# adaLN modulation on four column quarters of TensorE, and grouped small matmuls, in a two-layer token mixer

## The chip, the cores and the metric

One NeuronCore of one Trainium2 chip runs the whole program. The metric is the device time of one execution in microseconds. All engines of the core (TensorE for matmuls, VectorE, ScalarE, GpSimd, SyncE for DMA queues) run side by side, each through its own list of instructions in order.

## What is computed

The reference is a two-layer hybrid block on 256 context and 256 latent tokens of width 1024. In each layer a modulation vector is computed from the conditioning vectors, then four token mixers (retention, RG-LRU, gated DeltaNet, RWKV-7) run side by side on the normed and modulated stream, their outputs are merged through gates and an output matrix, and a SwiGLU feed-forward part follows:

```python
for l in range(DEPTH):                       # DEPTH = 2
    ml = jnp.split(cond_lat @ mod_w[l] + mod_b[l], 6, axis=-1)   # silu(c), 1024 -> 6 x 1024
    mc = jnp.split(cond_ctx @ mod_w[l] + mod_b[l], 6, axis=-1)
    pl = split_projection(modulate(rms_norm(h_lat, norm1_g[l]), ml[0], ml[1]) @ in_w[l])
    pc = split_projection(modulate(rms_norm(h_ctx, norm1_g[l]), mc[0], mc[1]) @ in_w[l])
    ...
    h_lat = h_lat + ml[2] * y_lat
    h_lat = h_lat + ml[5] * swiglu(modulate(rms_norm(h_lat, norm2_g[l]), ml[3], ml[4]), ...)
```

The modulation is thus a product of two columns (context, latent) with a 1024 x 6144 matrix per layer, in six parts q of 1024. Parts 0 and 1 are needed in the first norm, part 2 after the output matrix, 3 and 4 in the second norm, 5 after the feed-forward part.

## The kernel before

Dense weights come from HBM in units of 128 x 1024 fp32 (512 KB, tile `raw`, line 382, on SP's queue). ScalarE casts a unit to fp32r (`wh`, line 391) and VectorE subtracts (`wl`, line 352), and a block of 128 x 128 is then multiplied in three fp32r matmuls of 512 columns: wh with the high part of the activations, wh with the low part, wl with the high part (`dense`, `inp`). The activations lie transposed, channels on partitions, as XH and XL.

The tasks of each layer stand in lists written out by `_phases` (line 116). `first` holds the modulation needed at once, `seq1` the RWKV, retention and LRU work between projections and gates (`ga`), `seq2` the gated DeltaNet heads (`gd`) with the merges (`mg`), `seqo` the eight output blocks (`ow`), and `seqf` two times eleven feed-forward input steps (`fi`) and eight output blocks (`fo`). The program is emitted in that order. A scheduler then sets the order of each engine's list, from dependences, priorities and its own costs, so that pieces of one task stand among those of others; weight loads and splits are emitted with a higher priority (`early`) and go as far ahead as their buffers allow.

`mod` (line 569) does one half of a part q, 512 columns. Four halves at the start are done unsplit: eight fp32 matmuls with the two conditioning columns, padded to 32, as stationary operand (`sc32`) and the weights moving. All others are split: sixteen fp32r matmuls with `schl` stationary (hi and lo columns) and wh or wl moving. They occupy the first 32 columns of the array. A transpose on VectorE and five adds put the result into MODS. Two split halves stand in `seq1` (q=2), four in `seqo` (q=3, 4), fourteen in `seqf` of layer 0 (q=5, and all of layer 1). Every split half takes 4 units through the wh/wl path.

`rw_half` (line 707) does one RWKV pair of heads on 256 tokens: four small products with `sw` for decay and rate, then four chunks jj one after the other. In a chunk the state ST gives `pr` (tile ch), the inverse SF gives `pu`, then `uv` with `kt` gives the state's addition pS, and the output Y collects ST with RA and uv with sc. The two heads e and directions d give four small matmuls for each. `inv16` (line 667) inverts 16 x 16 triangular blocks by steps of shuffle, multiply and add on VectorE; `gd_head` (line 1001) calls it with two lanes, one for each direction. `params` (line 512 on) derives per-layer constants on VectorE, for both layers in the first phase.

Of the kernel before, what the change touches and what calls it, by code (L numbers as in the profile page):

```python
# [10 lines left out]
F32 = mybir.dt.float32  # L11
# [29 lines left out]
_GCOLS = [("triF", 128), ("triB", 128), ("aftF", 128), ("aftB", 128), ("gout", 256), ("s16", 32), ("nm0", 1), ("nm1", 1)]  # L41
# [13 lines left out]
def _consts():  # L55
# [14 lines left out]
    C["s16"][:, 0:16] = -1.0 * (r16 < c16)  # L70
    C["s16"][:, 16:32] = -1.0 * (r16 > c16)
    C["nm0"][:, 0] = -1.0 * ((p % 32) < 16)
    C["nm1"][:, 0] = -1.0 * ((p % 32) >= 16)
# [30 lines left out]
def _mod(l, *parts):  # L104
    return [("mod", l, q, c) for q in parts for c in range(2)]
# [10 lines left out]
def _phases(l):  # L116

    last = l + 1 == DEPTH
    first = [("mod", 0, q, c) for c in range(2) for q in range(2)] if l == 0 else []
    if last:  # L120
        seq1 = [("rws",), ("kvr", 0), ("kvr", 1), ("rw", 0), ("rt", 0), ("lr", 0), *_ga(3, 0, 2), ("kvr", 2), ("rw", 1), ("rt", 1), ("lr", 1), *_ga(3, 2, 4), ("kvr", 3), ("rw", 2), ("rt", 2), ("lr", 2), *_ga(3, 4, 6), ("rw", 3), ("rt", 3), ("lr", 3), *_ga(3, 6, 8)]
    else:
        seq1 = [("rws",), ("kvr", 0), ("kvr", 1), ("rw", 0), ("rt", 0), ("lr", 0), *_mod(0, 2), *_ga(3, 0, 2), ("kvr", 2), ("rw", 1), ("rt", 1), ("lr", 1), *_ga(3, 2, 4), *_ga(0, 0, 2), ("kvr", 3), ("rw", 2), ("rt", 2), ("lr", 2), *_ga(3, 4, 6), *_ga(0, 2, 4), ("rw", 3), ("rt", 3), ("lr", 3), *_ga(3, 6, 8), *_ga(0, 4, 8), *_ga(2, 0, 4)]
# [15 lines left out]
    seqo += []  # L139
    seqf += []  # L140
# [34 lines left out]
def _blocks(task, ahead):  # L175
# [6 lines left out]
    if k == "mod":  # L182
        _, l, q, c = task
        for kk in range(8):
            out += [(("mod_w", l), kk, slice(1024 * q + 512 * c + 128 * j, 1024 * q + 512 * c + 128 * j + 128)) for j in range(4)]
        return out
# [25 lines left out]
def _pack(inp):  # L212
# [36 lines left out]
    for n, (l, (m, kk, cols)) in enumerate(plan):  # L249
        w = f["mod_w"][m[1]] if isinstance(m, tuple) else mats[m][l]  # L250
        W[n // 8, :, n % 8, :] = w[128 * kk:128 * kk + 128, cols]
# [3 lines left out]
    for l in range(DEPTH):  # L255
# [7 lines left out]
        "W": W.reshape(nu, 128, 1024),  # L263
        "P": P,
# [6 lines left out]
class Kern:  # L271
    def __init__(self, ctx, tc, ap, out, dbg=None, depth=DEPTH, upto=None):
        self.ctx, self.tc, self.nc, self.ap, self.out = ctx, tc, tc.nc, ap, out
        self.dbgo, self.depth, self.upto = dbg or {}, depth, upto
        self.n = self.wi = self.nd = 0

# [67 lines left out]
    def mm(self, out, lhsT, rhs, start=True, stop=True, chk=False):  # L344
        self.nc.tensor.matmul(out=out, lhsT=lhsT, rhs=rhs, start=start, stop=stop, skip_group_check=chk)  # L345
# [32 lines left out]
    def raw(self, u, pool=None):  # L378
        pool = pool or self.wps[u % len(self.wps)]
        with self.early():  # L380
            raw = self.tl(pool, [128, 1024], "raw", bufs=self.nraw if pool is not self.wps[0] else 2)
# [81 lines left out]
    def setup(self):  # L463
# [36 lines left out]
        self.schl = self.cp.tile([128, 8, 64], F32R, name="schl")  # L500
        self.act(self.schl, self.kc[:, 0:1].unsqueeze(2).to_broadcast([128, 8, 64]), AF.Copy, scale=0.0)
        self.nc.scalar.copy(self.schl[:, :, 0:2], self.sc)
        self.nc.scalar.copy(self.schl[:, :, 32:34], self.sc)
        self.tt(self.schl[:, :, 2:4], self.sc, self.schl[:, :, 0:2].bitcast(F32), ALU.subtract)
# [6 lines left out]

    def params(self, l):
        nc = self.nc
        d = self.tl(self.cp, [128, 160], "dp", bufs=2)
# [5 lines left out]

        self.omu, self.hmu = col(15), col(15)
        self.ts(self.omu, self.p("mu", 0, 15), -1.0, 1.0, ALU.mult, ALU.add)
        self.ts(self.hmu, self.p("mu", 0, 15), 0.5)
# [45 lines left out]
    def mod(self, l, q, c, split=True):  # L569

        ps = self.psd()[0:32]
        for k in range(8):
            if not split:
                if k % 2 == 0:
                    u = self.wi // 8
                    _, raw = self.raw(u, self.wps[u % 3 != 2])
                    self.wi += 8
# [1028 lines left out]
```

## Time and profile before

| | us |
|---|---|
| runs of the kernel before: median (lowest, highest) | 2492.82 (2486.88, 2495.9) |
| the profiled execution, its own time | 2479.02 |
| span of the profiled execution | 2477.2 |
| TensorE busy, matmuls | 2358.9 |
| VectorE busy | 1767.9 |
| ScalarE busy | 1124.1 |

The span runs from the first to the last instruction in the profile; the execution's own time holds a little more. Busy TensorE time comes from modelled ends of matmuls that overlap, so the distance from start to start is what a matmul costs where the engine is full.

### The profile page before, as it was taken

What the parts mean: (1) busy time and instruction counts of PE and PEld (TensorE: products, weight loads), DVE (VectorE), ACT (ScalarE), POOL (GpSimd) and SP (SyncE); (2) the same over time, 40 slices, a digit from 0 to 9 for tenths busy, and PEclk for the clock granted to TensorE, in tenths of its full rate; (3) what the DMA queues carried; (4) which work ended last, traced back from release to release, by engine and by line L of the source; (5) the groups of instructions that cost most, each with busy time, mean ns of one, the idle gap of its engine ahead of it and who ended that gap; (6) DMA issues with size and microseconds to landing.
All of it is one profiled execution on the core that took longest, in us unless ns stands there. A gap on an engine that the chain in (4) does not pass through costs nothing. (4 is left out here: it accounts for less than half of the span.)

```text
span 2477.2 us, 48500 instructions
## 1 busy us (share of the span) xinstructions
PE 2358.9 (95%) x19016; PEld 1873.1 (76%) x19016; DVE 1767.9 (71%) x5357; ACT 1124.1 (45%) x2129; POOL 48.1 (2%) x146
## 2 busy tenths in 40 slices
PE   7999999999999999989999989999999999988998
PEld 2766777676877877667787877777777887888998
DVE  5787859685599965777635446978887688966555
ACT  3455445454444433444423224556564444544443
POOL 0000000000000000000000000000000000000000
PEclk9999999999999999999999999989999989989999
DMA  6214121212523243646635332212121432454553
GB/s 233 84 50 125 44 98 52 70 52 79 167 80 101 83 138 135 212 138 219 213 94 186 94 103 91 68 56 72 60 74 53 126 95 91 122 190 142 183 183 111
DMA packets 91381, 282.77 MB, mean 114 GB/s; under 512 B 10512, under 2 KB 21008, under 8 KB 90768
## 3 DMA queue, kind: packets, MB, share of 16 engines
q1 hardware_dynamic: 86256, 271.62, 34.2%
q10 hardware_dynamic: 4896, 8.05, 1.0%
q8 instruction: 150, 2.46, 0.4%
q14 instruction: 79, 0.65, 0.1%
HBM read 262.85 MB, written 16.78 MB: 113 GB/s over the span
## 5 line engine op out<-in xcount | busy, mean ns | idle before, releaser
L345 PE MATMUL d<-XH,wh 128*128 128x512 f32 (+1 forms) x2112 | 763.5, 363 | 22.9 <-ACT XH L342 10.8
L391 ACT CAST wh<-raw 128x1024 fp32r<-128x1024 f32 x436 | 452.2, 1048 | 721.8 <-PE d L345 473.8
L345 PE MATMUL d<-XL,wh 128*128 128x512 f32 (+1 forms) x2112 | 764.1, 362 | 2.9 <-DVE XL L359 2.9
L345 PE MATMUL d<-XH,wl 128*128 128x512 f32 (+1 forms) x2112 | 760.2, 360 | 0.8 <-DVE wl L352 0.8
L352 DVE TENSOR_TENSOR wl<-raw,wh 128x1024 fp32r<-128x1024 f32 x436 | 528.6, 1223 | 294.0 <-ACT wh L391 289.3
L345 PEld LDWEIGHTS d<-XH,wh 128*128 128x128 f32 x2112 | 403.0, 191 | 89.4 <-ACT XH L342 15.2
L345 PEld LDWEIGHTS d<-XL,wh 128*128 128x128 f32 x2112 | 404.0, 191 | 62.2 <-DVE XL L359 5.9
L345 PEld LDWEIGHTS d<-XH,wl 128*128 128x128 f32 x2112 | 404.3, 191 | 58.5 <-issue 7.5
L359 DVE SCALAR_TENSOR_TENSOR t<-t,d 128x512 f32<-128x512 f32 (+1 forms) x136 | 74.8, 551 | 83.8 <-PE d L345 75.3
L345 PE MATMUL d<-ih,wh 128*128 128x512 f32 (+1 forms) x352 | 118.3, 336 | 0.0
L345 PE MATMUL d<-il,wh 128*128 128x512 f32 (+1 forms) x352 | 118.3, 336 | 0.0
L345 PE MATMUL d<-ih,wl 128*128 128x512 f32 (+1 forms) x352 | 118.3, 336 | 0.0
L345 PE MATMUL d<-yh,wh 128*128 128x512 f32 (+1 forms) x256 | 92.1, 368 | 11.0 <-ACT yh L430 4.7
L345 PE MATMUL d<-yl,wh 128*128 128x512 f32 (+1 forms) x256 | 94.0, 368 | 3.2 <-DVE yl L352 3.2
L345 PE MATMUL d<-yh,wl 128*128 128x512 f32 (+1 forms) x256 | 91.2, 359 | 0.0
L359 DVE SCALAR_TENSOR_TENSOR H<-d,MOD,H 128x256 f32<-128x256 f32 x72 | 32.8, 479 | 55.2 <-PE d L345 55.0
L345 PEld LDWEIGHTS d<-ih,wl 128*128 128x128 f32 x352 | 66.8, 190 | 6.9
L345 PEld LDWEIGHTS d<-ih,wh 128*128 128x128 f32 x352 | 66.8, 190 | 6.9
L345 PEld LDWEIGHTS d<-il,wh 128*128 128x128 f32 x352 | 66.8, 190 | 6.8
L345 PE MATMUL d<-wh,schl 128*32 128x512 f32 x160 | 63.8, 400 | 2.1 <-DVE t L359 0.8
L345 PE MATMUL d<-wl,schl 128*32 128x512 f32 x160 | 65.4, 408 | 0.0
L345 PEld LDWEIGHTS d<-yh,wh 128*128 128x128 f32 x256 | 51.9, 206 | 16.7 <-ACT yh L430 5.7
(356 smaller groups left out, 3730.1 us busy)
## 6 DMA issues: line engine op xcount, KB each, us to landing
raw<-in_W_dram SPq DMA_DIRECT2D x452, 512.0 KB, 3.7
gd<-tm SPq DMA_DIRECT2D x20, 256.0 KB, 2.9
t<-gd SPq DMA_DIRECT2D x20, 256.0 KB, 4.2
yt<-yd SPq DMA_DIRECT2D x16, 256.0 KB, 4.5
H<-in_xT_dram ACTq DMA_DIRECT2D x8, 256.0 KB, 6.7
lrw<-in_LW_dram ACTq DMA_DIRECT2D x8, 256.0 KB, 2.6
yd<-tr SPq DMA_DIRECT2D x8, 256.0 KB, 3.4
H<-in_xT_dram SPq DMA_DIRECT2D x1, 2048.0 KB, 11.1
```

The lines of the kernel that those rows point to most:

```text
L345: self.nc.tensor.matmul(out=out, lhsT=lhsT, rhs=rhs, start=start, stop=stop, skip_group_check=chk)
L352: self.nc.vector.tensor_tensor(out=out, in0=a, in1=b, op=op)
L359: self.nc.vector.scalar_tensor_tensor(out=out, in0=a, scalar=s, in1=b, op0=op0, op1=op1)
L391: self.nc.scalar.copy(wh, r3)
```

## The change

The modulation is no longer split and no longer done in halves. A part q is eight steps k; a step loads 128 x 1024 fp32 of a repacked matrix WM (tile `mraw`, line 592, SP's queue), and four fp32 matmuls multiply 256 columns each, every one on its own 32 columns of the array and into its own 32 partitions of one PSUM tile (printed as `mg`). One transpose and one add end a part. The steps are grouped into tasks of n steps, and a new helper `gang` ties the matmuls of a task together: every later one of a group gets a dependence without a semaphore on the first, which is the one that is loaded last. The parts are placed anew: q=1, 0 and 2 in the first phase with a pool of 16 steps, q=3 and 4 as eight tasks of two steps after the output blocks with a pool of two steps, q=5 and layer 1's six parts as fourteen tasks of four steps in the feed-forward part with a pool of eight.

In `rw_half` the sw products write two PSUM tiles with both x side by side, and `gang` holds together sw, KB with RA, pr with ST's part of Y, pu, and pS with uv's part of Y. `gd_head` transposes the second direction's blocks first and runs one lane of eight blocks. Layer 1's parameters are loaded and derived at the sixth step of the feed-forward part, layer 0's after `rw_shared`, and the first few (`params_mu`) before it.

```diff
+def _mod(l, n, *parts):
+    return [("mod", l, q, k, n) for q in parts for k in range(0, 8, n)]
...
-    first = [("mod", 0, q, c) for c in range(2) for q in range(2)] if l == 0 else []
+    first = _mod(0, 1, 1, 0) + _mod(0, 4, 2) if l == 0 else []
...
-    mo = [] if last else _mod(0, 3, 4)
+    mo = [] if last else _mod(0, 2, 3, 4)
...
-    mf = [] if last else _mod(0, 5) + _mod(1, 0, 1, 2, 3, 4, 5)
+    mf = [] if last else _mod(0, 4, 5) + _mod(1, 4, 0, 1, 2, 3, 4, 5)
...
-            seqf += [("fi", f, j)] + mf[:1]
-            mf = mf[1:]
+            seqf += [("fi", f, j)]
+            if j and len(mf) > 2:
+                seqf += mf[:1]
+                mf = mf[1:]
         seqf += [("fo", f, m) for m in range(8)]
+    seqf += mf
...
     def mm(self, out, lhsT, rhs, start=True, stop=True, chk=False):
-        self.nc.tensor.matmul(out=out, lhsT=lhsT, rhs=rhs, start=start, stop=stop, skip_group_check=chk)
+        i = self.nc.tensor.matmul(out=out, lhsT=lhsT, rhs=rhs, start=start, stop=stop, skip_group_check=chk).ins
+        if self.ganged is not None:
+            if self.ganged:
+                self.tc.add_manual_dep(i, self.ganged[0].name, mybir.DependencyInfo(mybir.DependencyClass.NoSync, mybir.DependencyReason.DATA), reason="gang")
+            self.ganged.append(i)
...
+    def mod(self, l, q, k0, n):
+        W = []
+        for k in range(k0, k0 + n):
+            with self.early():
+                w = self.tl(self.mq, [128, 1024], "mraw")
+                self.nc.sync.dma_start(out=w, in_=self.ap["WM"][l, q, k])
+            W.append((k, w))
+        if k0 == 0:
+            self.mps = self.psm()
+        with self.gang():
+            for x, (k, w) in enumerate(W[::-1]):
+                for j in range(4):
+                    self.mm(self.mps[32 * j:32 * j + 32, 0:256], self.sc32[:, k], w[:, 256 * j:256 * j + 256],
+                            start=(k0 + x == 0), stop=(k0 + x == 7))
+        if k0 + n == 8:
+            t = self.t2(256)
+            self.nc.vector.transpose(out=t, in_=self.mps[:, 0:256])
+            self.tt(self.MODS[l][:, 8 * q:8 * q + 8, :], t.rearrange("p (m r) -> p m r", r=32)[:, :, 0:2],
+                    self.modb[:, l, 8 * q:8 * q + 8].unsqueeze(2).to_broadcast([128, 8, 2]), ALU.add)
...
+            with self.gang():
                 for d in range(2):
                     for e in range(2):
-                        self.mm(pS[E_[e], d], kt[:, d, jj, 64 * e:64 * e + 64], uv[:, jj, d, e])
+                        if not last:
+                            self.mm(pS[E_[e], d], kt[:, d, jj, 64 * e:64 * e + 64], uv[:, jj, d, e])
+                if out:
+                    for d in range(2):
+                        rv = slice(None, None, -1) if d else slice(None)
+                        t = slice(64 * ch(jj, d), 64 * ch(jj, d) + 64)
+                        for e in (1, 0):
+                            self.mm(Y[E_[e], t], uv[:, jj, d, e], sc[:, e, jj, d, 64:128][:, rv], start=False, stop=(jj == 3 and d == 1), chk=True)
...
-        self.inv16([(Nc[:, 0], Sc[:, 0], True), (Nc[:, 1], Sc[:, 1], False)], 4)
+        self.inv16([(U(Nc), U(Sc), True)], 8)
```

First place: SP's list at the start. `raw` is a unit of weights, `mraw` a step of the modulation. Before, the last units of the modulation, then the dense ones:

```order
L382 DMA raw_259<-in_W_dram 128x1024
L382 DMA raw_263<-in_W_dram 128x1024
L382 DMA raw_267<-in_W_dram 128x1024
L382 DMA raw_271<-in_W_dram 128x1024
L382 DMA raw_549<-in_W_dram 128x1024
L382 DMA raw_579<-in_W_dram 128x1024
L382 DMA raw_620<-in_W_dram 128x1024
```
Now the first rows, then the last step of q=0 with the first of q=2, then the last of q=2 with the dense units after it:

```order
L592 DMA mraw_155<-in_WM_dram 128x1024
L391 DMA raw_421<-in_W_dram 128x1024
L592 DMA mraw_162<-in_WM_dram 128x1024
L391 DMA raw_451<-in_W_dram 128x1024
...
L592 DMA mraw_276<-in_WM_dram 128x1024
L592 DMA mraw_344<-in_WM_dram 128x1024
...
L592 DMA mraw_375<-in_WM_dram 128x1024
L391 DMA raw_658<-in_W_dram 128x1024
L391 DMA raw_692<-in_W_dram 128x1024
```
Eight steps of q=2 moved in between q=0 and the dense units, and four dense units moved ahead, between the first steps.

Second place: TensorE's list in the second half of the first RWKV pair, where the chunk's uv is used (d is a dense PSUM tile, XH and XL the activations, x an LRU product, ch the state's addition). Before:

```order
L345 MATMUL d_2257<-XH,wh_2260 128x512
L345 MATMUL d_2257<-XL,wh_2260 128x512
L345 MATMUL Y_1628<-sc_1385,uv_1387 64x64
L345 MATMUL d_2257<-XH,wl_2261 128x512
L345 MATMUL d_2257<-XH,wh_2260 128x512
L345 MATMUL ch_1693<-uv_1387,kt_1386 64x64 x4
L345 MATMUL Y_1628<-sc_1385,uv_1387 64x64 x3
L345 MATMUL x_2140<-lrx_2050,lrw_2048 128x512
L345 MATMUL d_2257<-XL,wh_2260 128x512
```
And now at the same chunk:

```order
L343 MATMUL d_2119<-XL,wh_2122 128x512
L343 MATMUL d_2119<-XH,wl_2123 128x512
L343 MATMUL x_2098<-lrx_2008,lrw_2006 128x512
L343 MATMUL ch_1625<-uv_1345,kt_1344 64x64 x4
L343 MATMUL Y_1586<-sc_1343,uv_1345 64x64 x4
L343 MATMUL d_2153<-XH,wh_2156 128x512
L343 MATMUL d_2153<-XL,wh_2156 128x512
L343 MATMUL d_2153<-XH,wl_2157 128x512
```
The four products of Y, of which one stood apart from the others before, stand behind those of ch.

Third place: TensorE's list at the end of the output stage, and SP's within it. On TensorE the first row belongs to the last task of q=4; mg with a new number is q=5, st are the norm's row sums and their broadcast, d with XH the first feed-forward matmuls:

```order
L343 MATMUL mg_10639<-mraw_10771,sc_112 32x256 x4
L343 MATMUL mg_11053<-mraw_11051,sc_112 32x256 x4
L343 MATMUL mg_11053<-mraw_11049,sc_112 32x256 x4
L343 MATMUL mg_11053<-mraw_11047,sc_112 32x256 x4
L343 MATMUL mg_11053<-mraw_11045,sc_112 32x256 x4
L343 MATMUL mg_11053<-mraw_11144,sc_112 32x256 x4
L343 MATMUL mg_11053<-mraw_11142,sc_112 32x256 x4
L343 MATMUL mg_11053<-mraw_11140,sc_112 32x256 x4
L343 MATMUL mg_11053<-mraw_11138,sc_112 32x256 x4
L343 MATMUL st_10814<-cstt,t_1957_10791 128x1 x4
L343 MATMUL st_10835<-cstt,sm_10822 128x128 x4
L343 MATMUL d_10909<-XH,wh_10913 128x512
```
Eight steps of q=5, emitted among the feed-forward steps, stand ahead of the row sums (before, nothing stood between the last output block and the row sums).

On SP, where `mraw` with numbers from 11000 on belongs to the feed-forward part's pool, and mraw_10542 and 10544 to the second task of the output stage:

```order
L391 DMA raw_10694<-in_W_dram 128x1024
L592 DMA mraw_11045<-in_WM_dram 128x1024
L592 DMA mraw_11047<-in_WM_dram 128x1024
L592 DMA mraw_11049<-in_WM_dram 128x1024
L592 DMA mraw_11051<-in_WM_dram 128x1024
L391 DMA raw_10911<-in_W_dram 128x1024
L592 DMA mraw_11138<-in_WM_dram 128x1024
L592 DMA mraw_10542<-in_WM_dram 128x1024
L592 DMA mraw_11140<-in_WM_dram 128x1024
L592 DMA mraw_10544<-in_WM_dram 128x1024
```
The feed-forward part's steps stand between the output stage's loads, and ahead of some of them.

## Rows read from the trace of the kernel before

**Rows 1.** The page's first part: busy us, share of the span, instructions, by engine.
```profile
PE 2358.9 (95%) x19016; PEld 1873.1 (76%) x19016; DVE 1767.9 (71%) x5357; ACT 1124.1 (45%) x2129; POOL 48.1 (2%) x146
...
PEclk9999999999999999999999999989999989989999
```

**Rows 2.** Windows by stage: us, busy time and instructions by engine, clock, DMA share.
```profile
0.00:48.00 48.00, 35.24 (x82) 9.52 (x83) 22.56 (x127) 14.22 (x28) 0.77 (x6) 0.96 0.78 280
...
986.00:1050.00 64.00, 60.52 (x261) 43.14 (x260) 47.06 (x75) 30.69 (x34) 0.00 (x0) 1.00 0.63 209
1050.00:1060.00 10.00, 3.63 (x18) 3.04 (x18) 5.29 (x20) 1.88 (x4) 0.00 (x0) 0.74 0.01 4
1060.00:1227.00 167.00, 164.34 (x708) 119.95 (x708) 120.01 (x186) 81.75 (x101) 0.00 (x0) 0.98 0.59 194
1227.00:1476.00 249.00, 249.00 (x1099) 202.16 (x1098) 111.53 (x153) 72.34 (x84) 0.00 (x0) 1.00 0.37 119
1476.00:1487.00 11.00, 4.17 (x22) 3.29 (x20) 5.67 (x23) 3.10 (x10) 0.56 (x2) 0.75 0.70 261
```

**Rows 3.** TensorE's timeline around one split half: start, length, instruction, idle before.
```profile
1164.22 0.40 PE L345 MATMUL d<-wh,schl 128*32 128x512 f32 x1
...
1167.93 0.39 PE L345 MATMUL d<-XH,wh 128*128 128x512 f32 x1
```

**Rows 4.** Groups of instructions by line and form: busy us, mean ns, idle before.
```profile
L391 ACT CAST wh<-raw 128x1024 fp32r<-128x1024 f32 x436 | 452.2, 1048 | 721.8 <-PE d L345 473.8 <-issue 171.3 <-DMA raw<-in_W_dram 63.7
L345 PEld LDWEIGHTS d<-wh,schl 128*32 128x32 f32 x160 | 17.4, 109 | 20.6 <-issue 2.0 <-DVE t L359 1.2 <-ACT wh L391 1.0
```

**Rows 5.** Timelines of the start, TensorE and VectorE.
```profile
16.54 7.05 PE L345 MATMUL d<-raw,sc 128*32 128x512 f32 x16 [0.81 <-DMA raw<-in_W_dram]
...
40.49 3.62 PE L345 MATMUL d<-raw,sc 128*32 128x512 f32 x8
...
44.70 0.70 DVE L587 STREAM_TRANSPOSE t<-d 32x512 f32<-32x512 f32 x1
...
47.64 0.63 PE L345 MATMUL d<-XH,wh 128*128 128x512 f32 x1 [3.53 <-ACT XH L342]
...
67.32 0.47 PE L345 MATMUL d<-XH,wh 128*128 128x512 f32 x1 [2.21 <-DVE tm L359]
```

**Rows 6.** Timeline of an RWKV chunk on the two column halves, loads and matmuls.
```profile
165.59 0.31 PEld L345 LDWEIGHTS ch<-uv,kt 128*64 128x64 f32 x8 [0.33 <-DVE cB L678]
165.59 0.45 PE L345 MATMUL ch<-uv,kt 128*64 128x64 f32 x8
...
165.88 0.40 PE L345 MATMUL Y<-sc,uv 128*64 128x64 f32 x8
```

**Rows 7.** TensorE's timeline at a Y product that stands alone.
```profile
564.08 0.40 PE L345 MATMUL d<-XH,wl 128*128 128x512 f32 x1
564.41 0.33 PE L345 MATMUL Y<-sc,uv 128*64 128x64 f32 x2
564.66 0.50 PE L345 MATMUL d<-XH,wh 128*128 128x512 f32 x1
```

**Rows 8.** Window of the loads at the start, columns as in rows 2.
```profile
5.00:30.00 25.00, 20.37 (x38) 4.50 (x39) 8.15 (x38) 6.27 (x17) 0.00 (x0) 0.95 1.03 394
```

**Rows 9.** VectorE's timeline in `inv16`: two lanes of DeltaNet, then one lane of RWKV.
```profile
696.37 0.17 DVE L678 STREAM_SHUFFLE cB<-gS 128x8 f32<-128x8 f32 x1
...
696.99 0.17 DVE L678 STREAM_SHUFFLE cB<-gS 128x12 f32<-128x12 f32 x1
...
130.17 0.18 DVE L678 STREAM_SHUFFLE cB<-cS 128x16 f32<-128x16 f32 x1
...
130.81 0.19 DVE L678 STREAM_SHUFFLE cB<-cS 128x24 f32<-128x24 f32 x1
```

**Rows 10.** Timeline of the norm before the feed-forward part: the row sums.
```profile
1052.64 1.05 PE L345 MATMUL st<-cstt,t 128*128 128x1 f32 x8 [2.42 <-DVE t L352]
```

**Rows 11.** DMA issues of the output stage: count, KB each, median us to landing.
```profile
raw<-in_W_dram SPq DMA_DIRECT2D x25, 512.0 KB, 4.7
```

More of the change, by code (lines that the diff above doesn't have):

```diff
@@ L380, in raw @@
         with self.early():
-            raw = self.tl(pool, [128, 1024], "raw", bufs=self.nraw if pool is not self.wps[0] else 2)
+            raw = self.tl(pool, [128, 1024], "raw", bufs=2)
             self.nc.sync.dma_start(out=raw, in_=self.ap["W"][u])
@@ L567, in params @@
         self.pars.append({n: getattr(self, n) for n in names.split()})
[L569 to L577, printed above, removed]
-                self.mm(ps, self.sc32[:, k], raw[:, 512 * (k % 2):512 * (k % 2) + 512], start=(k == 0), stop=(k == 7))
-                continue
-            for j in range(4):
-                self.wblock()
-            a = 4 * (k % 2)
-            wh, wl = (t[:, a:a + 4, :].rearrange("p a b -> p (a b)") for t in self.wcur)
-            self.mm(ps, self.schl[:, k, 0:32], wh, start=(k == 0), stop=False)
-            self.mm(ps, self.schl[:, k, 32:64], wl, start=False, stop=(k == 7))
-        t = self.t2()[0:32]
-        self.nc.vector.transpose(out=t, in_=ps)
-        t4 = t.rearrange("p (m a j) -> p m a j", a=4, j=32)
-        m = 8 * q + 4 * c
-        for a in range(4):
-            self.tt(self.MODS[l][32 * a:32 * a + 32, m:m + 4, :], t4[:, :, a, 0:2], t4[:, :, a, 2:4], ALU.add)
-        m = self.MODS[l][:, m:m + 4, :]
-        self.tt(m, m, self.modb[:, l, 8 * q + 4 * c:8 * q + 4 * c + 4].unsqueeze(2).to_broadcast([128, 4, 2]), ALU.add)
@@ L1119, in gd_head @@
                     self.mm(ps[r, d, u], X[r, d, u], S32[r, d, u])
-        self.tt(S32, S32, ps, ALU.add)
-        T2 = q2()
-        nc.vector.transpose(out=fl(T2), in_=fl(S32))
+        TI, T2 = q2("i32", 1), q2("t32", 1)
+        for d, t, x in ((0, TI, T2), (1, T2, TI)):
+            self.tt(t[:, d], S32[:, d], ps[:, d], ALU.add)
+            nc.vector.transpose(out=f1(x[:, d]), in_=f1(t[:, d]))
         SF = self.tl(gp, [128, 2, 4, 128], "sf", bufs=nb)
@@ L1547, in layer @@
         with ExitStack() as es:
+            if not lat:
+                es.enter_context(self.mod_stream(f"mqf{l}", 8))
             es.enter_context(self.more_weights(f"wf{l}"))
@@ L1555, in layer @@
                     j = t[2]
+                    if not lat and t[1:] == (0, 5):
+                        self.load_params(l + 1)
+                        self.params_mu()
+                        self.params(l + 1)
+                        self.__dict__.update(self.pars[l])
                     if j == 0:
```

186 lines of the change are left out of this document (89 added, 97 removed).

## The prediction

> **What bounds the kernel now.** I read the page's engine shares first, then the windows by stage, then timelines of the places that the diff touches. TensorE is busy for 2358.9 of 2477.2 us at a granted clock near full speed in almost every slice, and VectorE for 71% [rows 1]. So a change pays where it takes passes off TensorE in a full stage, or where it shortens one of the few gaps. The windows say which stages are full [rows 2]: in the feed-forward part of layer 0 (1060 to 1476 us) TensorE is busy for 413.3 of 416 us, in the output stage (986 to 1050) for 60.5 of 64. The gaps are the start (35.2 of 48 us), the norm before the feed-forward part (3.6 of 10) and the norm before layer 1 (4.2 of 11). The timed runs have a median of 2492.82, the profiled execution 2479.02: I make the sum against the profiled span of 2477.2 and add 2 us for what lies around it and 14 for the median.
>
> **What one modulation costs today.** A split half takes 16 matmuls from 1164.22 to 1167.93, that is 3.71 us with the next dense matmul directly behind [rows 3]. Twenty such halves are spread over the program: 2 in the first sequence, 4 in the output stage, 14 in the feed-forward part. In a full stage each is worth its 3.71 us, 14 x 3.71 = 52 in the feed-forward part alone. That the halves need no wh/wl splits any more (80 of the 436 casts of 1.05 us, as many subtracts) I cost at nothing [rows 4]: ScalarE is 45% busy [rows 1], and TensorE hides both engines.
>
> **What one costs after: the unknown.** A whole part q is now 8 steps k, and a step is four fp32 matmuls of 256 columns, each on its own quarter of the array's columns. An fp32 matmul is two passes: at the start, 16 passes of 512 columns last 7.05 us and 8 last 3.62 [rows 5], so a pass starts every 3.43 / 8 = 0.43 us. A pass of 256 columns alone thus starts every 0.215 us. Call p the time from pass to pass when all four quarters are used. No row shows four quarters at full depth. Its ends: 0.054 (0.215 / 4, all four at once) and 0.215 (one after the other). The nearest row is the RWKV product on the two column halves: 8 passes of 64 columns start at 165.59, the next group at 165.88, so 0.29 us [rows 6]. Alone, each would need 0.43 x 64 / 512 = 0.054, 8 of them 0.43. So halves do run side by side, with a small group's entry in the 0.29, and I take p = 0.054: full depth, 128 rows, as there, and only the number of column groups is further. A group in dense work pays the change of array form at both ends, about 0.1 us each way: dense to Y is 0.33 [rows 7] where a step in a full stretch is 3.71 / 16 = 0.23 [rows 3]. That makes a feed-forward task (4 steps, 32 passes) 32 x 0.054 + 0.3 = 2.0 us, and an output task (2 steps, 16 passes) 0.86 + 0.25 = 1.1.
>
> **The sum, by place.**
>
> Start. Today the fp32 halves on TensorE set it: their last transpose starts at 44.70 and the first dense matmul at 47.64 [rows 5]. Afterwards their passes are a quarter and the loads decide. The last step of q=0 is the 16th mraw, behind four raw units and the 2 MB of H: 20 x 0.524 + 2.1 = 12.6 MB. At the 394 GB/s of the start [rows 8] that is 32 us, from about 3 us on: 35, plus half a microsecond of passes, one transpose and one add. That is 8 us earlier than now. Ends: -13 (H and mraw share better than thought, and the one add replaces five small ones), -3 (norm held by VectorE's layer parameters, which are still issued early). The third q, 64 passes or 3.5 us, lies among dense matmuls that wait for the norm: nothing, and 3.5 if they don't. Its eight loads, 4.2 MB, come forward on SP ahead of the fifth raw unit, which lands near 46 us instead of 35. The first pair of projection tiles (two units) lasts from 47.64 to 67.32 today [rows 5], paced by the norm, and four units lie ahead of the 24 steps: nothing, and up to 3 if the norm gets faster than that. The bytes of the modulation stay the same.
>
> Parameters. Layer 1's move from the first norm to the sixth step of the feed-forward part, where VectorE is busy for 120 of 167 us [rows 2]: nothing. Without that room a block of them would hold the gate products of one step for a few us.
>
> First sequence. Two halves go, 7.4 us at most. Take -6, since that stage waits a little on its chains; ends -7.4 and -3.
>
> RWKV grouping. Today the order tears 44 of the Y groups: one product goes alone into the dense matmuls and three follow. Such a detour costs 0.58 (564.08 to 564.66) where 0.23 would do, 0.35 [rows 7], and the group that is then whole is longer by two passes of 0.29 / 8, 0.07 [rows 6]: 44 x 0.28 = 12. The sw products stand in 39 places before and some 24 after: 15 x 0.2 = 3. So -15 if TensorE is the limit throughout, 0 if the chain of chunks behind it is; in the stages where this stands TensorE is nearly full (95% over the whole span [rows 1]), so I take two thirds, -10.
>
> DeltaNet's joined inverse. Two lanes of four blocks step in 0.62 us (696.37 to 696.99), one lane of eight in RWKV in 0.64 (130.17 to 130.81) [rows 9]. The chain does not change its length, and the copies and transposes about cancel: 0, ends -4 and +4.
>
> Output stage. Four halves (14.8) become eight tasks of 1.1 (8.8): -6. Of the 3.5 us of gaps there [rows 2] about one goes with the lighter splitting: -7. Ends -9 and, where loads come late (below), +4.
>
> Feed-forward. -52 for the 14 halves, +20 for the ten tasks among dense work. The other four stand in the two norms, between the last dense matmul and the row sums: TensorE has 2.42 us free there [rows 10], two tasks need 3.4 + 0.3, so 1.3 late each time, +3. Together -29; ends -34 and the rivals.
>
> Sum: -8 - 6 - 10 + 0 - 7 - 29 = -60. Span 2417, profiled 2419, median **2433**.
>
> **Rivals.**
>
> Two wide: only two quarters run at once, p = 0.107. Ten tasks 37, the norms 2 x 4.8 = 10: feed-forward -5. Output tasks 1.95 x 8 = 15.6: 0. Sum -8 - 6 - 10 + 0 - 5 = -29: median 2464. For it: halves are the most that a row shows. Against it: nothing in those rows hints at a limit of two.
>
> Serial, the slower one: the quarters share all 128 rows, so the moving data of one blocks the others, p = 0.215. Feed-forward 72 + 24 - 52 = +44, output 8 x 3.7 - 14.8 = +15, start: the gain goes (27.5 us of passes as today) and the third q's 13.8 us come partly on top, +8. Sum 44 + 15 + 8 - 6 - 10 = +51: median 2544. It decides from about p = 0.15. Against it stand the halves of [rows 6], which share their rows too.
>
> Weights not hidden: a quarter's weight load waits until the pass in the same rows has ended. A load of this shape lasts 0.109 [rows 4], so p = 0.163; against p = 0.054 that adds 0.109 to 320 + 128 + 128 passes, 63, and some 4 at the start: +7, median 2500. Against it: loads (8 of them) and passes of the two halves start together at 165.59, the loads last 0.31 us and the next group starts 0.29 later [rows 6], so the two lie beside each other. [...]
>
> Late loads in the output stage: its pool holds two steps, so the loads of a task wait on SP for the task before it, and the feed-forward part's loads are mixed in between on the same queue. One output block, 24 x 0.23 = 5.5 us, is the time they have. The median load there lands in 4.7 us [rows 11], two with a stranger between them in 6 to 8 by my estimate. Seven waits of up to 2 us cost up to 14: -46, median 2447.
>
> Chains decide in RWKV: the 10 vanish, median 2443.
>
> **Chances.** Four wide with all or most of the rest 0.63; two wide 0.16; late loads or chain-bound RWKV 0.08; weights not hidden 0.06; serial 0.07. About 0.5%, 12 us, is what a measurement of this kernel can tell from no change, so the line to "same" is at 2480: the first three are faster (0.87), the fourth is the same (0.06), the last slower (0.07). The range reaches from the best ends (-13 - 7 - 15 - 4 - 9 - 34 = -82, median 2411, and 5 for what I have not seen) to the two-wide case and some of its own late loads: 2406 to 2470.
>
> **What would show it.** In the profile after: a feed-forward task's first pass to the next dense matmul in 2.0 us (3.7 two wide, 5.5 with loads not hidden, 7.2 serial); the first dense matmul near 39.5 instead of 47.64; Y always x8, and the sequences shorter by more than the halves; output stage near 57 us with no TensorE wait named on mraw; feed-forward about 384 for 416; row sums in the norm about 1 us later after the last dense matmul. The prediction is wrong if p is over 0.1, if the output stage waits on mraw, or if the RWKV stages keep their length.

## The result, and the profile after

The changed kernel takes 2420.47 us in the median of 4 runs (2415.91 to 2424.22), the kernel before beside it 2489.85: a ratio of 0.972, 95% interval 0.969 to 0.976. The forecast was 2433, range 2406 to 2470. The profiled execution took 2415.91, its span is 2414.1, 63.1 us less than before.

The page of the changed kernel, engine shares and granted clock:

```profile
PE 2283.1 (95%) x19400; PEld 1830.6 (76%) x19400; DVE 1625.6 (67%) x4644; ACT 1033.4 (43%) x2014; POOL 56.0 (2%) x154
...
PEclk9999999999999999989999999999999899998999
```

Against [rows 1], TensorE has 75.8 us less to do and is as full as it was; VectorE lost 142 us and ScalarE 91. Where the time went is read from one landmark in TensorE's timeline to the next: the first dense matmul with XH, the first of a merge (yh), the first and last with mh, the first of the feed-forward part, its last with ih, and the same in layer 1. The distances in us, each between two starts of the profiled execution:

| | before | after | difference | forecast |
|---|---|---|---|---|
| start, to the first dense matmul | 47.6 | 44.8 | -2.8 | -8 |
| first sequence, layer 0 | 631.0 | 612.1 | -18.9 | -6 and a half of -10 |
| DeltaNet and merges, layer 0 | 308.4 | 306.9 | -1.5 | 0 |
| output stage, layer 0 | 62.9 | 50.9 | -12.0 | -7 |
| norm before the feed-forward part | 9.9 | 23.0 | +13.1 | +1.3 |
| feed-forward part | 416.9 | 393.5 | -23.4 | -32 |
| norm before layer 1 | 10.3 | 22.1 | +11.8 | +1.3 |
| first sequence, layer 1 | 446.3 | 434.4 | -11.9 | a half of -10 |
| DeltaNet, merges and output stage, layer 1 | 328.8 | 314.3 | -14.5 | 0 |
| rest | 215.1 | 212.3 | -2.8 | 0 |

The sum is the forecast's within about 3 us, but four terms carry a larger gain than foreseen and the two norms a loss of 25.

TensorE's timeline around one task of the feed-forward part, which answers to [rows 3]:

```profile
1089.15 0.39 PE L343 MATMUL d<-XH,wl 128*128 128x512 f32 x1
1089.47 1.93 PE L343 MATMUL mg<-mraw,sc 128*32 128x256 f32 x32
1091.33 0.50 PE L343 MATMUL d<-XH,wh 128*128 128x512 f32 x1
```

and one task of the output stage:

```profile
1010.54 1.07 PE L343 MATMUL mg<-mraw,sc 128*32 128x256 f32 x16
```

From 1089.47 to 1091.33 are 1.86 us for 32 passes. The group of 16 of the output stage lasts 1.07 and that of 32 lasts 1.93, so 16 more passes cost 0.86, 0.054 each: all four quarters at once, the lower end of p. In the records of the single passes the four quarters start some 7 ns apart, and each quarter starts its next pass 0.215 us later. Entering costs 0.1 (0.32 instead of 0.23 behind the dense matmul), as in [rows 7].

The same stretches by windows (columns as in [rows 2]): the output stage, the norm, the feed-forward part up to 1182 us, and at last the norm before layer 1:

```profile
950.00:1015.00 65.00, 65.00 (x347) 49.02 (x345) 21.85 (x32) 12.43 (x14) 0.00 (x0) 1.00 0.63 218
1015.00:1037.60 22.60, 10.05 (x97) 6.18 (x96) 14.18 (x54) 7.01 (x15) 0.00 (x0) 0.72 0.83 303
1037.60:1182.00 144.40, 141.79 (x752) 107.57 (x752) 64.33 (x131) 41.45 (x59) 0.00 (x0) 0.97 0.53 179
...
1431.00:1453.00 22.00, 8.00 (x83) 5.58 (x81) 10.11 (x31) 6.53 (x17) 0.57 (x2) 0.66 0.35 124
```

The output stage is full now: the gaps of 3.5 us that it had in [rows 2] went too. The norms are the new holes, 12.6 and 14 us of idle TensorE.

TensorE in the second norm of layer 0, then in the first norm of layer 1:

```profile
1014.66 0.39 PE L343 MATMUL d<-mh,wl 128*128 128x512 f32 x1
1017.65 1.63 PE L343 MATMUL mg<-mraw,sc 128*32 128x256 f32 x16 [2.60 <-DMA mraw<-in_WM_dram]
1019.84 4.42 PE L343 MATMUL mg<-mraw,sc 128*32 128x256 f32 x64 [0.55 <-DVE t L603]
1029.62 0.59 PE L343 MATMUL st<-cstt,t 128*128 128x1 f32 x2 [5.36 <-DVE t L361]
...
1431.39 3.66 PE L343 MATMUL mg<-mraw,sc 128*32 128x256 f32 x64
1445.24 1.87 PE L343 MATMUL st<-cstt,t 128*128 128x1 f32 x8 [10.19 <-DVE t L361]
```

The row sums (st) come 15 and 14 us after the last dense matmul where [rows 10] had 2.4 us free, and the modulation's own matmuls are over 5 and 10 us before them. The sums wait for VectorE's t, the added squares. ScalarE's timeline shows why, first before the feed-forward part, then before layer 1:

```profile
1008.14 1.05 ACT L400 CAST wh<-raw 128x1024 fp32r<-128x1024 f32 x1 [12.41 <-PE d L343]
1009.10 0.62 ACT L340 ACTIVATE t<-H 128x512 f32<-128x512 f32 x1
1020.94 1.04 ACT L400 CAST wh<-raw 128x1024 fp32r<-128x1024 f32 x1 [11.21 <-DMA raw<-in_W_dram]
...
1425.83 1.05 ACT L400 CAST wh<-raw 128x1024 fp32r<-128x1024 f32 x1 [9.82 <-PE d L343]
1435.12 0.34 ACTq L1489 DMA_DIRECT2D csd<-in_csd_dram  x1
1435.50 3.75 ACT L340 ACTIVATE t<-H 128x512 f32<-128x512 f32 x7 [8.61 <-PE mg L343]
```

The squares of H (t<-H, eight in a norm) come in one block at the end. In the kernel before, the last ones came one by one, each after its output block, and one was left at the end:

```profile
1045.79 0.63 ACT L342 ACTIVATE t<-H 128x512 f32<-128x512 f32 x1
1051.23 0.63 ACT L342 ACTIVATE t<-H 128x512 f32<-128x512 f32 x1 [4.81 <-DVE H L359]
```

In front of the block stands a cast that waits for late weights, or a DMA issue that waits for the modulation's matmuls. Whether these are the cause is what the experiments have to tell.

VectorE at the start, which answers to the transpose in [rows 5]:

```profile
42.75 0.25 DVE L365 TENSOR_SCALAR dp<-dp 128x8 f32<-128x8 f32 x2
42.91 0.44 DVE L603 STREAM_TRANSPOSE t<-mg 128x256 f32<-128x256 f32 x1
```

The transpose of q=0 stands behind the end of a parameter chain (dp). In VectorE's list 21 of the 26 instructions that write dp, for both layers, lie ahead of it: although layer 1's are written at the sixth feed-forward step, the scheduler put most of them at the start.

### The profile page after: what moved, and what is told of

Its sections match the earlier page's. It is cut to its first block, busy times and chain, and to the rows that moved or that the text cites. A ratio compares the mean times of both kernels' runs of the same rounds, so it can differ in the third digit from the quotient of the medians.

```text
span 2414.1 us, 48292 instructions
## 1 busy us (share of the span) xinstructions
PE 2283.1 (95%) x19400; PEld 1830.6 (76%) x19400; DVE 1625.6 (67%) x4644; ACT 1033.4 (43%) x2014; POOL 56.0 (2%) x154
## 5 line engine op out<-in xcount | busy, mean ns | idle before, releaser
L400 ACT CAST wh<-raw 128x1024 fp32r<-128x1024 f32 x356 | 372.8, 1048 | 746.2 <-PE d L343 437.1
L361 DVE TENSOR_TENSOR wl<-raw,wh 128x1024 fp32r<-128x1024 f32 x356 | 435.1, 1223 | 355.1 <-ACT wh L400 350.3
L343 PE MATMUL mg<-mraw,sc 128*32 128x256 f32 x768 | 55.7, 420 | 21.9 <-DMA mraw<-in_WM_dram 16.0
L343 PEld LDWEIGHTS mg<-mraw,sc 128*32 128x32 f32 x768 | 23.0, 116 | 50.3 <-DMA mraw<-in_WM_dram 22.4
```

What stands on the lines that cost most here:

```text
L343: i = self.nc.tensor.matmul(out=out, lhsT=lhsT, rhs=rhs, start=start, stop=stop, skip_group_check=chk).ins
L361: self.nc.vector.tensor_tensor(out=out, in0=a, in1=b, op=op)
L400: self.nc.scalar.copy(wh, r3)
```

## The experiments

Each kernel is timed beside the kernel before on the same chip; the medians of before lay between 2487.7 and 2490.8, so the medians of different experiments can be set side by side to about 3 us. A stage of one profile moves by more than that with the granted clock, as layer 1 will show (434.5 us at 0.97 and 442.0 at 0.95 with one list but for a place): where a stage is compared, its clock has to be looked at too.

**One part undone at a time.** The first has the RWKV and DeltaNet functions of before, the second only the RWKV one, the third only the DeltaNet one:

```diff
-        with self.gang():
-            for x, src in enumerate((self.rth, self.rad)):
...
+        for x, (src, P) in enumerate(((self.rth, pw), (self.rad, pa))):
...
-        self.inv16([(U(Nc), U(Sc), True)], 8)
+        self.inv16([(Nc[:, 0], Sc[:, 0], True), (Nc[:, 1], Sc[:, 1], False)], 4)
```

> The changed kernel with the RWKV and DeltaNet functions of before: only the modulation and the parameters are new. Theory A (each part works where it stands): the start -3, the first sequence -7 for its two halves, the output stage -12, the two norms +13 and +12, the feed-forward part -23, and layer 1 from its first dense matmul on as before: -20, so about 2470. Rival B (the 38 us that layer 1 lost come from what the modulation and the parameters left behind, such as lighter ScalarE and VectorE): layer 1 keeps -30 or more, about 2435.

Measured 2467.25, ratio 0.991 (0.988 to 0.995). Layer 1's first sequence is 455.7 us here and its DeltaNet to output stage 333.2, no shorter than before. So theory A: the modulation by itself is worth 23 us of the 69, and layer 1's gain is not its. The 23 is a low figure: layer 1's first sequence is 9.4 us longer than before, though TensorE's list there is the old one but for a place or two in 4581; the granted clock is 0.93 in it (1470 to 1926 us), 0.96 before (1487 to 1933 us).

> The changed kernel with only the RWKV half pair as before. Theory A (grouping the small matmuls saves TensorE time wherever it is full): both first sequences longer by 10 to 12 us each, 2440 to 2445. Rival B (the chain of chunks sets the pace and the grouping is hidden): within 4 us of the changed kernel, 2416 to 2425.

Measured 2450.44, 0.986 (0.982 to 0.989): 30 us over the changed kernel, more than A asked. First sequences 622.6 and 453.5, so 10.5 and 19.1 of it. The windows of both first sequences, here and then in the changed kernel:

```profile
45.00:668.00 623.00, 614.97 (x5394) 446.86 (x5395) 442.16 (x1325) 299.59 (x594) 16.44 (x51) 1.00 0.25 78
1455.00:1908.80 453.80, 430.25 (x4523) 330.73 (x4523) 366.72 (x1239) 244.50 (x503) 14.68 (x44) 0.94 0.22 66
```
```profile
45.00:657.00 612.00, 601.82 (x5394) 445.53 (x5394) 442.44 (x1323) 298.55 (x593) 16.45 (x51) 0.99 0.26 79
...
1453.00:1887.50 434.50, 412.15 (x4580) 319.82 (x4581) 364.30 (x1235) 244.90 (x510) 15.88 (x44) 0.97 0.24 71
```

About the same instructions keep TensorE busy for 13.2 and 18.1 us less, and the stages are shorter by about that (11.0 and 19.3). The idle time stays: no chain swallowed the gain.

The two layers are not alike, though. TensorE's list changes 1232 times between dense matmuls (those that write d) and others with the old function, and 1112 times with the new; of these 120 changes 96 lie in layer 0's first sequence and 24 in layer 1's. In layer 0 a change is thus worth 10.5 / 96 = 0.11 us, about what each end of a group in dense work costs (0.32 and 0.33 where a step takes 0.23, around the task above). In layer 1 the 24 can't carry 19.1 us. There the granted clock differs: 453.8 us at 0.94 and 434.5 at 0.97 are 427 and 421 us of full clock, so by this estimate some 14 of the 19.1 are the clock's and 5 the list's, and the grouping by itself is worth about 15 of the 30. The old function does not set that clock alone: the kernel before has it too, with the same list but for a place or two, and stands at 0.96 and 446.3 us. Why the clock differs stays open.

> The changed kernel with only the DeltaNet head as before. Theory A (as predicted, the joined inverse is worth nothing): within 4 us of the changed kernel. Rival B (the 15 us that the second sequence of layer 1 lost between its start and the output stage are the joined inverse's): 2434 to 2437, nearly all of it in layer 1, and in layer 0 under 3 us.

Measured 2435.90, 0.981 (0.977 to 0.984): 15.4 us over the changed kernel, rival B. Layer 1 from its first merge to the last output block takes 330.9, with the joined inverse 314.3; in layer 0 it is 309.7 against 306.9. The stretch of the first three heads in layer 1, from the first inverse to the end of the third, in the kernel before, then in this one, both with two lanes, then with one lane (changed kernel):

```profile
1991.00:2132.00 141.00, 126.29 (x1307) 111.54 (x1306) 123.38 (x605) 63.92 (x159) 3.00 (x9) 0.94 0.34 102
```
```profile
1950.00:2091.00 141.00, 125.52 (x1305) 110.14 (x1303) 123.15 (x602) 63.95 (x159) 3.00 (x9) 0.94 0.35 102
```
```profile
1946.00:2072.00 126.00, 117.89 (x1378) 105.45 (x1377) 115.12 (x425) 61.92 (x153) 4.75 (x11) 1.00 0.38 116
```

TensorE is idle for 15.5 us with two lanes and for 8.1 with one: half of the 15 us. The other half is busy time, 125.5 and 117.9 us, with a granted clock of 0.94 and 1.00. VectorE is busy for 123 us with 602 instructions, or for 115 with 425. The run puts back the whole head function, but what the count lost is the inverse's own: 45 each of mask loads, shuffles and adds and 44 multiplies fewer; the rest about cancels. Two of TensorE's waits with two lanes:

```profile
1972.21 0.39 PE L345 MATMUL d<-yh,wh 128*128 128x256 f32 x1 [3.02 <-DVE zs L370]
...
2020.48 0.47 PE L345 MATMUL d<-XH,wh 128*128 128x512 f32 x1 [3.24 <-DVE t L370]
```

It waits for work of VectorE that is not the inverse's and that stands in VectorE's list just behind the last steps of an inverse (zs starts at 1971.74, t at 2019.93). The granted share in the clock's records of that stretch is 0.5 from 1973.4 and 2021.2, soon after these two waits, and from 1990.4, after one of 1.26 us, for 17 us in all, and so it is for 17 us of the stretch in the kernel before (from 2013.9, 2031.0 and 2061.7); in the changed kernel it stays at 1 in its stretch. VectorE's timeline inside one step of the joined lane:

```profile
1991.13 0.18 DVE L690 STREAM_SHUFFLE cB<-gS 128x16 f32<-128x16 f32 x1
1991.21 0.41 DVE L361 TENSOR_TENSOR M<-M,t 128x256 f32<-128x256 f32 x1
1991.55 0.17 DVE L361 TENSOR_TENSOR cB<-cB,gN 128x16 f32<-128x16 f32 x1
```

A shuffle and its multiply lie 0.42 us apart, and 0.34 of that is the merge's add, which is other work. The three instructions of a step depend on each other; with two lanes the other lane's three lie in between. So the lane is not shorter (from the first shuffle to the last, the first two heads take 23.1 and 24.2 us with two lanes, 28.5 and 31.7 with one), but what shares VectorE with it gets on. That this is the cause is read from these rows; no run changed VectorE's order alone.

**The pass on four quarters.** The matmuls of a task in the order quarter by quarter:

```diff
-            for x, (k, w) in enumerate(W[::-1]):
-                for j in range(4):
+            for j in range(4):
+                for x, (k, w) in enumerate(W[::-1]):
```

> The changed kernel with the matmuls of a task in another order: all steps of one column quarter, then the next quarter, instead of all four quarters of a step. The same instructions and loads. Theory A (a pass of 0.215 us is divided by four only where the neighbours in the list stand on other quarters): a task of four steps needs 6.9 us instead of 2.0, one of two steps 3.4 instead of 1.1: 10 x 5 + 8 x 2.3 + two norms with 5 each, less what stays hidden, about +75, 2485 to 2505. Rival B (TensorE brings passes on different quarters together wherever they stand in the list): within 4 us of the changed kernel.

Measured 2454.41, 0.988 (0.984 to 0.991): 34 us over the changed kernel, between the two. The feed-forward part is 26 us longer. One task:

```profile
1096.85 4.59 PE L343 MATMUL mg<-mraw,sc 128*32 128x256 f32 x32
1101.38 0.50 PE L343 MATMUL d<-XH,wh 128*128 128x512 f32 x1
```

32 passes in 4.53 us, where the mixed order takes 1.86 and one after the other would take 32 x 0.215 = 6.9. So passes of the next quarter do overlap with those before them, but only some: in the records of the single passes a quarter's eight start 0.215 us apart, and the next quarter starts 0.89 us behind the one before, with its fifth pass. A list that alternates the quarters is needed for the full gain.

**The norms.** Four kernels ask what holds the squares. In the first, the last two tasks go back into the feed-forward part:

```diff
-            if j and len(mf) > 2:
+            if j and mf:
```

> The last two modulation tasks go back among the feed-forward steps instead of behind the last output block. Theory A (they delay the norm of layer 1 by 12 us, because its squares on ScalarE stand behind a DMA issue that waits for the tasks): the norm's gap is 10 us again, two tasks cost 2.0 each in dense work, so -8: about 2412. Rival B (the gap has another cause, and the tasks were free there): +4, about 2424.

Measured 2408.03, 0.968 (0.966 to 0.971): 12 us under the changed kernel. The norm before layer 1 takes 10.8 us instead of 22.1 and the feed-forward part 4.0 more. So it is the place of the two tasks, as A has it; it does not yet say by which wait.

In the second, every cast of weights that follows in the program is held behind the norm's last square:

```diff
-            self.nc.scalar.copy(wh, r3)
+            i = self.nc.scalar.copy(wh, r3).ins
+            if self.sqlast is not None:
+                self.tc.add_manual_dep(i, self.sqlast.name, NoSync, reason="sq")
```

> The casts of the feed-forward part's first weights stand behind the norm's squares on ScalarE. Theory A (the second norm of layer 0 got 13 us longer since the squares waited for a cast whose weights were late): the squares follow the output blocks again, the row sums come right behind the eight steps of q=5, about 5 us earlier: 2414 to 2417. Rival B (the matmuls of q=5, which wait for loads ahead of the row sums, hold the norm by themselves): within 2 us of the changed kernel.

Measured 2419.02, 0.973 (0.969 to 0.976), the same as the changed kernel. The norm is 23.4 us, with no cast in front of the squares; the profile now has a square wait 23.46 us for the add that follows the modulation's transpose. So the late weights, which the profile names as the releaser, are not the cause: without them another wait ends just as late. It is not rival B's either, since the third kernel moves the tasks away and keeps the gap. That kernel has the two changes above (the last tasks back in the feed-forward part, the casts behind the squares), the held parameters of the next part, and each feed-forward task held behind the dense matmuls ahead of it. It shows the wait:

> All three, and the tasks of the feed-forward part held behind the dense matmuls that precede them in the program, so that none stands in the norms. Theory A (the two norms' 25 us are waits of ScalarE's list and of matmuls ahead of the row sums): both norms near 11 us, four tasks of 2.0 more in dense work, start -3: 2420 - 12 - 11 + 8 - 3 = 2402. Rival B (in the second norm the late weights themselves are the limit, with or without the squares): its gap stays above 18 us, 2409 or more.

Measured 2413.90, 0.971 (0.966 to 0.975). Before the feed-forward part 22.7 us, although no task of q=5 stands there; before layer 1 12.2. The numbers are rival B's, but the squares do not wait for weights. ScalarE and VectorE in the norm before the feed-forward part:

```profile
1016.39 0.45 DVE L618 STREAM_TRANSPOSE t<-mg 128x256 f32<-128x256 f32 x1 [2.81 <-PE mg L345]
1016.88 0.17 DVE L369 TENSOR_TENSOR MOD<-t,modb 128x16 f32<-128x16 f32 x1
1017.08 0.63 ACT L650 ACTIVATE t<-H 128x512 f32<-128x512 f32 x1 [22.91 <-DVE MOD L369]
```

ScalarE stood for 22.91 us until the add that reads the modulation's transpose. It computes nothing with that. But the transpose's t and the squares' t come from one ring of six tiles (`t2`), and a square that gets the transpose's place has to wait until the add has read it. With eight tasks behind eight output blocks, q=4's transpose comes after the last block, and three of the squares here, seven of the eight in the changed kernel, come after it.

The fourth kernel gives the transpose a tile of its own, from the pool of the modulation's loads, and nothing else:

```diff
-            t = self.t2(256)
+            t = self.tl(self.mq, [128, 256], "mt", bufs=1)
```

> One thing only: the modulation's transpose writes a tile of its own instead of one from the ring of six that the norm's squares use. Theory A (the squares of both norms waited for a ring tile, which the last part's transpose had not given back, so they came after it in one block): the squares follow the output blocks one by one again; second norm of layer 0 23 to about 15, first norm of layer 1 22 to about 13, together -15 to -18: 2403 to 2406. Rival B (late weights on ScalarE's list, as the look at the changed kernel alone suggested): both gaps stay, within 3 us of the changed kernel.

Measured 2410.72 (2394.59 to 2414.48), 0.968 (0.964 to 0.972). The squares follow the output blocks again, by ScalarE's timeline:

```profile
1009.65 0.63 ACT L340 ACTIVATE t<-H 128x512 f32<-128x512 f32 x1 [6.01 <-DVE H L368]
...
1016.38 0.64 ACT L340 ACTIVATE t<-H 128x512 f32<-128x512 f32 x1
1023.22 0.63 ACT L340 ACTIVATE t<-H 128x512 f32<-128x512 f32 x1 [6.20 <-DVE H L368]
```

The two norms take 14.4 and 11.8 us instead of 23.0 and 22.1: 19 us, a little more than theory A's 15 to 18. So the ring is the cause in both. But only 10 of them are in the median, and its interval overlaps that of the changed kernel. In this profile the start is 3.2 us later, with VectorE's list there ordered anew, and the first sequences are 3.2 and 7.6 us longer. In layer 1 that is not the list: of 4580 matmuls one stands elsewhere. The window of that sequence:

```profile
1447.40:1889.40 442.00, 419.88 (x4604) 328.07 (x4605) 361.13 (x1235) 243.26 (x506) 15.93 (x44) 0.95 0.24 71
```

The granted clock is 0.95, in the changed kernel 0.97 (above): 442.0 and 434.5 us are 420 and 421 of full clock, so by the same estimate the 7.6 are the clock's. The fastest of the four executions, 2394.59, has the highest mean clock, 0.984 where the others have 0.977 to 0.979. Why the clock differs with the same list stays open.

**The parameters.** The instructions of `params` are held behind the norm that precedes them in the program, by dependences without a semaphore on VectorE's and ScalarE's last instruction of the norm:

```diff
     def params(self, l):
         nc = self.nc
+        self.behind = self.normed
...
+    def pin(self, e, i):
+        if self.behind is not None:
+            self.tc.add_manual_dep(i, self.behind[e].name, NoSync, reason="pin")
```

> The derived parameters of both layers are held behind the norm that precedes them in the program; in the changed kernel the scheduler put both layers' chains in front of the first norm. Theory A (the chains on VectorE held the transpose of q=0 from about 39 to 42.9 us): first dense matmul 3 us earlier, about 2417. Rival B (the loads hold the transpose): no change at the start; or the gain goes again where the chains now stand, 2419 to 2422.

Measured 2414.29, 0.971 (0.968 to 0.974), not told apart from the changed kernel by the intervals. In the profile the first dense matmul is 2.5 us earlier, 42.3, and the first sequence, where the chains now stand, 2.5 longer. So A is right on the start, and B on what it is worth.

**The RWKV function shared out.** Only the sw products as before, without the group:

```diff
-        with self.gang():
-            for x, src in enumerate((self.rth, self.rad)):
...
+        for x, (src, P) in enumerate(((self.rth, pw), (self.rad, pa))):
...
+                self.mm(P[d], sw[64 * d:64 * d + 64, x, :], src[64 * d:64 * d + 64, T])
```

> The changed kernel with only the sw products of the RWKV half pair as before (two PSUM tiles for each x, in the old order); pr, pu, pS and Y stay grouped. It shares out the 30 us that the RWKV function is worth. Theory A (as the prediction priced it, Y is the larger share, sw a fifth): up to 6 us over the changed kernel, 2422 to 2427. Rival B (the start of a half pair, where ScalarE waits for sw, is the tight place): 10 us or more over it, 2430 or above.

Measured 2423.46, 0.974 (0.971 to 0.976): 3 us over the changed kernel, theory A, and not told apart from it by the intervals. So sw's share is small; the rest of what the function is worth is in the grouping of KB with RA, pr, pu, pS and Y.

**A version that beats both.** The tile of its own, the last two tasks among the feed-forward steps and the held parameters; then the same with a modulation task ahead of its output block:

```diff
-        seqo += [("ow", m)] + mo[m:m + 1]
+        seqo += mo[m:m + 1] + [("ow", m)]
```

> The tile of its own, the last two tasks among the feed-forward steps, and the parameters held behind the norm. Theory A: both norms near 11 to 13 us, feed-forward +4, start -3: 2420 - 11 - 10 + 4 - 3 to -6 = 2395 to 2400. Rival B (what one of them gives the other has given already): no better than 2403.

Measured 2401.98, 0.966 (0.964 to 0.968); norms 16.0 and 11.3. A is right on the second of them only, and the total lies between the two theories, 2 us over A's and 1 under B's: they are not told apart.

> As the one before, and a modulation task of the output stage stands ahead of its output block instead of behind it, so that the last one has a block's time more. Theory A (the 2.6 us that TensorE waits for the last task's loads after the last block go): 2 to 3 us under the one before. Rival B (the pool of two steps makes the loads late anyway): the same within 2 us.

Measured 2397.05 (2396.57 to 2403.67), 0.965 (0.962 to 0.968), the fastest kernel here: its interval lies under that of the changed kernel, but overlaps that of the one before. Norms 11.4 and 11.2. The reason is not A's, though: the wait for q=4's last load is still there. TensorE in the second norm of layer 0, in the kernel tried just before this one and then in this one:

```profile
1021.84 1.93 PE L344 MATMUL mg<-mraw,sc 128*32 128x256 f32 x16 [2.87 <-DMA mraw<-in_WM_dram]
1023.71 1.87 PE L344 MATMUL st<-cstt,t 128*128 128x1 f32 x8
1025.50 6.46 PE L344 MATMUL mg<-mraw,sc 128*32 128x256 f32 x64
1031.89 1.16 PE L344 MATMUL st<-cstt,sm 128*128 128x128 f32 x8
```
```profile
1018.60 1.07 PE L344 MATMUL mg<-mraw,sc 128*32 128x256 f32 x16 [2.60 <-DMA mraw<-in_WM_dram]
1019.61 1.39 PE L344 MATMUL st<-cstt,t 128*128 128x1 f32 x8
1020.92 3.21 PE L344 MATMUL mg<-mraw,sc 128*32 128x256 f32 x32
1024.07 1.16 PE L344 MATMUL st<-cstt,sm 128*128 128x128 f32 x8
1025.16 1.91 PE L344 MATMUL mg<-mraw,sc 128*32 128x256 f32 x26
```

There the broadcast of the row sums (st<-cstt,sm) stands behind all 64 passes of q=5, here behind 32 of them; the other 32 come after it, beside the norm's work on VectorE. VectorE's chain between the two (st to sm) also holds two splits of weights there, 1.23 and 1.22 us long, and none here. How the 4.6 us of the norm divide between these was not tried.

Against the kernel that the change started from it is 3.5% faster, against the changed one some 23 us.

## Why the prediction was right, point by point

**The unknown, p.** Right: four quarters run at once, 0.054 us a pass, 1.86 us a task for a forecast of 2.0. The two-wide and the serial rival fall with it. So does the one in which the weight loads are not hidden, by which a task would have taken 5.5: 32 loads, of 0.110 us each in the median, lie within the 1.86 us of one task on the same rows, the first from 1089.47, the last to 1090.92.

**Start.** -2.8 for -8, at the low end of the range. What that end named, "norm held by VectorE's layer parameters, which are still issued early", is what the rows at 42.75 and 42.91 show, and it is worth 2.5 us. Even without the chains the first matmul comes at 42.3, not 39.5. Most of the rest is in the loads: the last step of q=0 lands at 37.74 us in the changed kernel and at 37.54 with the chains held back, where 35 was reckoned.

**First sequence, the two halves.** -6 forecast; with the modulation alone the stage is 3.6 shorter. Within the stated ends (-7.4 and -3).

**RWKV grouping.** -10 forecast, 30 measured, of which about 15 at the same clock. The mechanism was right. The term took a third off for chains, which took nothing: the -15 of its other end is what the lists are worth. That it is 30 by the runs comes from the clock in layer 1, which the forecast did not have.

**DeltaNet's joined inverse.** 0 forecast, 15 measured, outside the stated end of -4. The step that failed is "The chain does not change its length", as the reason for 0: it priced a step of the lane by itself, and what the lane leaves of VectorE to others was not priced. The stretch in layer 1, where with two lanes VectorE is 87% busy, TensorE idle for 15 of 141 us and its clock at 0.94, could have been read in the kernel before by windows, and was not.

**Output stage.** -12 for -7: all 3.5 us of gaps went, where about one was taken (that the lighter splitting did it was not tried); and the last of the eight tasks lies behind the last block and so in the next row. The rival of late loads, one of the signs named against the prediction, came true for this one task, 2.60 us in the norm.

**Feed-forward and norms.** The ten tasks were right: -23.4 is 28.6 over the pure -52, of which the tasks are 10 x 2.1 = 21. That leaves 7.6, and it lies in the dense matmuls, which the forecast took as unchanged. TensorE's timeline inside a dense block, before and then after, two matmuls that lie 18 steps apart:

```profile
1095.65 0.39 PE L345 MATMUL d<-XH,wh 128*128 128x512 f32 x1
...
1099.73 0.39 PE L345 MATMUL d<-XH,wh 128*128 128x512 f32 x1
```
```profile
1095.63 0.39 PE L343 MATMUL d<-XH,wh 128*128 128x512 f32 x1
...
1099.84 0.39 PE L343 MATMUL d<-XH,wh 128*128 128x512 f32 x1
```

18 steps take 4.08 us and then 4.21, so one takes 0.227 and 0.234. The feed-forward part has 1056 matmuls with XH or XL, and 1056 x 0.007 is 7.4. The four tasks in the norms failed: +1.3 each by TensorE's free 2.42 us, +13.1 and +11.8 measured. The step took TensorE's own gap for the price. What the tasks delay is a tile of a ring, and through it the squares on ScalarE.

So the total was right with errors of both signs, which is luck: 25 us lost in the norms, where 3 were allowed for, and 5 at the start, and 9 less gained in the feed-forward part, against 20 and 15 more in RWKV and DeltaNet. The median is lower than forecast by 12.5 us mainly since 14 were added to the profiled execution for it, where 4.6 were measured.

## What to carry to other kernels

When work is moved into a gap, look beyond the engine that has the gap: which tiles of shared rings does it take, and who gets them next. A releaser in the trace names the wait that ended last; take it away, and look whether the time falls before the story is believed. Look at the granted clock of a stage (0.95 and 0.97 for 442.0 and 434.5 us) before its length is put down to the list. And a chain on an engine that is 87% busy is priced by the slots it takes as well as by its length.

## What was not expected of the hardware

The same dense matmul with XH or XL and 512 columns starts every 0.227 us before and every 0.234 after (rows above); in the lists by quarters, which have the new modulation too, 18 steps take 4.20 us (1084.16 to 1088.36), 0.233 each. Matmuls of 512 columns with ih, il, mh or ml keep their spacing, 0.227 in the median before and after. The cause stays open.

TensorE overlaps passes on different column quarters even where its list does not alternate them, but in part: 4.53 us for 32 passes, between the 1.86 of the mixed order and the 6.9 reckoned for one after the other.

Layer 1's first sequence took 446.3, 455.7 and 453.5 us with one list on TensorE but for a place or two (the kernel before, the modulation alone, the RWKV function of before), at granted clocks of 0.96, 0.93 and 0.94. In the first three heads of layer 1 the granted clock was 0.94 with 15.5 us of idle time in 141 and 1.00 with 8.1 in 126. In the norms of the changed kernel it was 0.72 and 0.66, and the 64 passes of q=5 there took 4.42 and 3.66 us where 64 x 0.054 is 3.46.
